# RWKV-7 units of a hybrid decoder block: the products of the two heads are issued in turn

## The chip, the cores and the metric

The kernel runs on one core of a Trainium2 chip. The metric is the device time of one launch in microseconds (us): the median of repeated runs, 2375.93 us before the change (three runs, 2375.08 to 2376.63). All views below come from one profiled execution, which took 2376.5 us. In them PE is the tensor engine (TensorE), PEld its weight loads, DVE the vector engine (VectorE), ACT the scalar engine (ScalarE), POOL is GpSimd, and SP the engine that issues most loads.

## What is computed

One layer of a decoder on a sequence of 512 tokens with 2048 features, in float32. The normalised input is projected by one large matrix; its columns belong to four groups of token mixers: four gated DeltaNet heads (A), four retention heads (B), eight Mamba-2 heads (C) and eight RWKV-7 heads of width 64 (D). The outputs are joined, projected back, and a squared-ReLU MLP follows. The change concerns group D alone:

```python
def _rwkv7_scan(r, decay, k, v, kk, a):
    def step(S, inp):
        r_t, d_t, k_t, v_t, kk_t, a_t = inp
        sa = jnp.einsum('bhvk,bhk->bhv', S, -kk_t)
        S = S * d_t[:, :, None, :] + sa[..., None] * (kk_t * a_t)[:, :, None, :] + v_t[..., None] * k_t[:, :, None, :]
        return S, jnp.einsum('bhvk,bhk->bhv', S, r_t)
    xs = tuple(jnp.moveaxis(t, 1, 0) for t in (r, decay, k, v, kk, a))
    _, y = lax.scan(step, jnp.zeros((Bsz, H, N, N), jnp.float32), xs)
    return jnp.moveaxis(y, 0, 1)
```

## The kernel before

**Stages.** The projection and the token mixers run together until about 890 us; then come the output projection, the two halves of the MLP (each by a scheme with seven block products in place of eight), and the last normalisation. The change is in the first stage.

**Units.** The mixers are cut into twelve units, run in the order D0, A0, D1, A1, C0, D2, A2, C1, D3, A3, B0, B1. A D unit (function `rwkv`) has two RWKV heads: head 0 lies on partitions 0 to 63 of its tiles, head 1 on 64 to 127 (`half`; `rb` is the pair the other way round). The 512 tokens are eight chunks of 64.

**What sets the order.** Each projection block (`proj`) is 48 products of 128x512 (L457), each operand split in two parts, hi and lo (L281 on ScalarE, L282 on VectorE). Every unit is a generator. After every four L457 products (`QUANTUM`) one tick passes; a `yield n` in a unit that has got all its projections means that its next piece comes n ticks later. So TensorE's order is written by hand: pieces of up to two older units stand between the projection products of the next. GpSimd's order is written by hand too. The orders of VectorE, ScalarE and of the load queue are made by a list scheduler from the dependencies, so a change of the program's order can move instructions there.

**Accumulators.** `BK()` gives one of six rotating accumulators (`bk`, `zb`, `xb`, `sb`, `yb`), one bank of 128x512 each; the two accumulators of the projection are apart.

**A D unit behind its projections, with the lines of the profile:** the keys of both heads are transposed, eight per head, into one accumulator per head (L652) and copied by ScalarE to `KT` (L654). Then the products of keys and queries, four chunks to an accumulator (L665), are masked by VectorE into `Ph` (L666), scaled and masked again (L674, L675), and reduced (L679). A recursion of fifteen steps on VectorE (L567 to L569) and a few small products (L692, L713, L720, with L700, L704 and L705 on VectorE between them) invert a triangular matrix. Last comes the loop over chunks: `zb` is the sum of a product with the state `Sx` (L732) and one with `Ph` (L733), copied to `Z` (L734); `xb` (L738) gives the update (L739, L740), `sb` (L749) the new state `Sn` (L752, L754), and `yb` is the sum of L757 and L759, copied to `Y` (L760). In the first chunk there is no state, so L732 and L759 are missing.

**How products stand on the array.** The profile gives rows*columns of the array that a product uses. L652 and L665 use 64 rows (those of the head's partitions) and all 128 columns; L732, L733, L738, L759 and L692 use 64*64; L749 and L757 128*64. A transpose is one record in the profile, a product of float32 operands two.

Of the kernel before, what the change touches and what calls it, by code (L numbers as in the profile page):

```python
# [191 lines left out]
def tile_trunk(ctx: ExitStack, tc: tile.TileContext, ins, out):  # L192
    nc = tc.nc
    V, A, PE, G = nc.vector, nc.scalar, nc.tensor, nc.gpsimd
# [13 lines left out]
    M = lambda n="m": ps.tile([128, 1024], F32, tag="m", name=n, bufs=NM)  # L208
    BK = lambda n="bk": pm.tile([128, 512], F32, tag="bk", name=n)
# [14 lines left out]
    def C(n, a=0, w=None):  # L224

        if n in _L:
            if n not in wide:
                wide[n] = S(n)
                nc.scalar.dma_start(wide[n], ins["wide"][_L.index(n)])
            return wide[n][:, a:a + (w or 512)]  # L230
        return con[:, _C[n][0] + a:_C[n][0] + a + (w or _C[n][1])]
    Pm = lambda n, a=0, w=1: par[:, _P[n][0] + a:_P[n][0] + a + w]

    def bc(ap, shape):
        return ap.broadcast_to(shape)
# [93 lines left out]
    def weights(more=0):  # L329
        ahead(more)  # L330
        w = halves.pop(st["n"])
        st["n"] += 1
        return w
# [239 lines left out]
    def rwkv(j):  # L573
        v3 = lambda q: q.rearrange("p (c t) -> p c t", c=8)
        half = (slice(0, 64), slice(64, 128))
# [4 lines left out]
        bk = BK()  # L580
# [14 lines left out]
        bk = BK()  # L595
# [13 lines left out]
        bk = BK()  # L609
# [11 lines left out]
        AR = M("AR").rearrange("p (c x t) -> p c x t", c=8, x=2)  # L621
        KB = M("KB").rearrange("p (c x t) -> p c x t", c=8, x=2)
# [11 lines left out]
        bk = BK()  # L634
# [7 lines left out]
        bk = BK()  # L642
# [3 lines left out]
        yield 4  # L646

        KT = []
        for h in range(2):
            bk = BK()  # L650
            for c in range(8):
                PE.transpose(bk[:, 64 * c:64 * c + 64], KB[half[h], c], C("i2")[half[h]])  # L652
            kt = v3(S("KT"))
            A.copy(kt, v3(bk))  # L654
            KT.append(kt)
            yield 1

        Ph = []
        for h in range(2):
            p = M("Ph").rearrange("p (c x t) -> p c x t", c=8, x=2)  # L660
            for q in range(2):
                bk = BK()
                b4 = bk.rearrange("p (c x t) -> p c x t", c=4, x=2)
                for c in range(4):
                    PE.matmul(b4[:, c], KB[half[h], 4 * q + c], AR[half[h], 4 * q + c], start=True, stop=True)  # L665
                V.tensor_tensor(p[:, 4 * q:4 * q + 4].rearrange("p c x t -> p c (x t)"),  # L666
                                bk.rearrange("p (c y) -> p c y", c=4),
                                bc(C("rmask").unsqueeze(1), (128, 4, 128)), op=ALU.mult)
                yield 1
            Ph.append(p)  # L670
        rb = (half[1], half[0])
        cm = S("cm")
        for h in range(2):
# [14 lines left out]
        def quad(fn_l, fn_r):  # L688
            bk = v3(BK())
            for c in range(8):  # L690
                for h in range(2):
                    PE.matmul(bk[rb[h], c], fn_l(h, c), fn_r(h, c), start=True, stop=True)  # L692
            return bk
# [4 lines left out]
        bk = quad(lambda h, c: Ph[h][rb[h], c, 0], lambda h, c: X[rb[h], c])  # L698
# [11 lines left out]
        bk, U = v3(BK()), v3(S("U"))  # L710
# [6 lines left out]
        bk = v3(BK())  # L717
# [9 lines left out]
        for c in range(8):  # L727
            Z = E128("Z")[:, 0:64]
            zb = BK("zb")
            for h in range(2):  # L730
                if Sx is not None:
                    PE.matmul(zb[rb[h], 0:64], AR[half[h], c, 0], Sx[half[h]], start=True, stop=False)  # L732
                PE.matmul(zb[rb[h], 0:64], Ph[h][half[h], c, 0], VX[h][half[h], c], start=Sx is None, stop=True)  # L733
            V.tensor_copy(Z, zb[:, 0:64])  # L734
            yield 1
            xb = BK("xb")
            for h in range(2):
                PE.matmul(xb[rb[h], 0:64], XT[rb[h], c], Z[rb[h]], start=True, stop=True)  # L738
            A.activation(VX[0][64:128, c], xb[64:128, 0:64], AF.Copy, scale=nn2[64:128, c:c + 1])  # L739
            V.tensor_scalar(VX[1][0:64, c], xb[0:64, 0:64], nn2[0:64, c:c + 1], None, op0=ALU.mult)  # L740
            if c < 7 and Sx is not None:
                sg = E128("sg")[:, 0:64]
                V.tensor_scalar(sg, Sx, gc[:, c:c + 1], None, op0=ALU.mult)
            yield 2
            Sn = None
            if c < 7:
                sb = BK("sb")
                for h in range(2):
                    PE.matmul(sb[half[h], 0:64], KT[h][:, c], VX[h][:, c], start=True, stop=True)  # L749
                Sn = E128("Sn")[:, 0:64]  # L750
                if Sx is None:
                    V.tensor_scalar(Sn, sb[:, 0:64], gc[:, c:c + 1], None, op0=ALU.mult)  # L752
                else:
                    V.scalar_tensor_tensor(Sn, sb[:, 0:64], gc[:, c:c + 1], sg, op0=ALU.mult, op1=ALU.add)  # L754
            yb = BK("yb")
            for h in range(2):
                PE.matmul(yb[half[h], 0:64], Ph[h][:, c, 1], VX[h][:, c], start=True, stop=Sx is None)  # L757
                if Sx is not None:
                    PE.matmul(yb[half[h], 0:64], AR[half[h], c, 1], Sx[half[h]], start=False, stop=True)  # L759
            A.copy(Y[:, c], yb[:, 0:64])  # L760
            Sx = Sn
            yield 1
# [18 lines left out]
        bk = BK()  # L781
# [402 lines left out]


    units = {"D": rwkv, "A": gdn, "C": ssd, "B": ret}
    active = []

# [284 lines left out]
    for j in range(2 * EARLY):  # L1473
        p, m = j // 2, 1 + j % 2
        h, l = weights(2)
# [205 lines left out]
    for c in range(7):  # L1681
        for s in range(2):
            for m in DORD[c]:
# [3 lines left out]
                for t in range(2):  # L1687
                    if m in (2, 3, 4):
                        x = ht[t + 2 * (m == 4)][s + 2 * (m == 3)]
                    else:  # L1690
                        x = kept[m, s, t]
# [28 lines left out]
    c = 7  # L1720
# [49 lines left out]
```

## Time and profile before

| | |
|---|---|
| median of three runs | 2375.93 us |
| profiled execution | 2376.5 us |
| its span, first to last instruction | 2374.7 us |
| TensorE busy, of the span | 98% |
| VectorE busy, of the span | 75% |
| ScalarE busy, of the span | 43% |
| granted TensorE clock, mean | 0.993 |
| L665, 128 records: busy | 18.5 us |
| L652, 64 records: busy | 5.7 us |
| L757 and L759, 128 and 112 records: busy | 18.5 and 18.2 us |
| L732 and L733, 112 and 128 records: busy | 9.5 and 9.4 us |

A timeline row has the start in the span, the time to the end of the last of the row's instructions, engine, line, operation, output<-inputs, rows*columns of the array, elements, type and count, and in brackets the engine's idle time before it with what ended that. Records of TensorE overlap, so the step from one row's start to the next is what it occupies. A row of the groups has the busy time of all its instructions, the mean of one in ns, and the idle time before them. A busy time is what at least one of the group's instructions covers.

### The profile page before, as it was taken

The page shows a single profiled execution, that of the slowest core. Times are in us where ns is not written, and L with a number is a line of the kernel's source. Part 1 is how long each engine was busy: PE and PEld are TensorE (multiplying, and loading weights), DVE is VectorE, ACT ScalarE, POOL GpSimd, SP SyncE. Part 2 cuts the span into 40 slices and gives each one's busy share as a digit, 9 for nine tenths or more (in the row PEclk, how much of TensorE's full clock was granted, in tenths as well). Part 3 has the DMA queues.
Part 4 walks back from the last instruction along what each step waited for, and adds up shares of the span by engine and source line. Part 5 has one row for each costly group of instructions (what it writes and reads, how often), then busy time and mean ns, then how long its engine had stood idle before and what let it go on. Part 6 is the DMA issues. An engine that isn't in the chain of part 4 may idle for free.

```text
span 2374.7 us, 36713 instructions
## 1 busy us (share of the span) xinstructions
PE 2317.4 (98%) x14690; PEld 1988.6 (84%) x14690; DVE 1773.4 (75%) x2783; ACT 1016.3 (43%) x1480; POOL 195.4 (8%) x270
## 2 busy tenths in 40 slices
PE   6999999999999999998999999999999999999996
PEld 6777778777777788878999999999988888888885
DVE  5685855775584444468888888888888888898898
ACT  5322233333322232354455555555565544445443
POOL 1110201211210210011111100000010000000000
PEclk9999999999999999999999999999999999999998
DMA  5553626563653675564877754444476655656451
GB/s 199 147 142 82 161 70 153 150 159 98 168 144 98 173 195 195 176 218 158 260 216 213 222 160 160 160 160 160 160 276 218 205 169 169 212 174 212 151 199 71
DMA packets 159916, 404.76 MB, mean 170 GB/s; under 512 B 12929, under 2 KB 79489, under 8 KB 158721
## 3 DMA queue, kind: packets, MB, share of 16 engines
q1 hardware_dynamic: 83952, 285.42, 36.9%
q0 software_dynamic: 38912, 77.08, 14.3%
q10 hardware_dynamic: 36880, 39.92, 4.9%
q8 instruction: 115, 1.88, 0.3%
q14 instruction: 57, 0.46, 0.1%
HBM read 355.70 MB, written 113.77 MB: 198 GB/s over the span
## 4 chain that ended last, share of the span: by engine, by line
PE 80%; DVE 9%; issue 6%; DMA 2%; POOL 1%; ACT 1%; SPq 0%; POOLq 0%; DVEq 0%; ACTq 0%
PE acc L457 17%; PE p L1441 8%; PE p L1443 8%; PE p L1442 8%; PE dn L1675 8%; PE dn L1676 8%; PE dn L1674 8%; PE wo L1239 2%; PE wo L1247 2%; PE wo L1240 2%; DVE lo L282 1%; PE acc L481 1%; DVE xi L567 1%; DVE xm L568 1%; DVE lo L1575 1%
## 5 line engine op out<-in xcount | busy, mean ns | idle before, releaser
L1574 ACT CAST hi<-raw 128x1024 fp32r<-128x1024 f32 x224 | 235.0, 1054 | 290.6 <-PE dn L1676 238.2
L1674 PE MATMUL dn<-hi,x 128*128 128x512 f32 x896 | 349.8, 390 | 5.7 <-ACT hi L1574 5.7
L1675 PE MATMUL dn<-lo,x 128*128 128x512 f32 x896 | 350.0, 391 | 2.4 <-DVE lo L1575 2.2
L1676 PE MATMUL dn<-hi,x 128*128 128x512 f32 x896 | 349.3, 390 | 0.0
L281 ACT CAST hi<-raw 128x1024 fp32r<-128x1024 f32 x162 | 169.7, 1049 | 409.5 <-PE acc L457 307.6
L457 PE MATMUL acc<-ah,hi 128*128 128x512 f32 x832 | 336.3, 404 | 0.0
L457 PE MATMUL acc<-al,hi 128*128 128x512 f32 x832 | 335.5, 403 | 0.0
L457 PE MATMUL acc<-ah,lo 128*128 128x512 f32 x832 | 333.7, 401 | 0.0
L1575 DVE TENSOR_TENSOR lo<-raw,hi 128x1024 fp32r<-128x1024 f32 x224 | 272.9, 1223 | 62.6 <-ACT hi L1574 62.2
L1434 ACT CAST hi<-raw 128x1024 fp32r<-128x1024 f32 x216 | 226.6, 1051 | 209.7 <-PE p L1442 149.1
L1435 DVE TENSOR_TENSOR lo<-raw,hi 128x1024 fp32r<-128x1024 f32 x216 | 263.0, 1222 | 70.9 <-ACT hi L1434 70.4
L282 DVE TENSOR_TENSOR lo<-raw,hi 128x1024 fp32r<-128x1024 f32 x160 | 195.3, 1223 | 142.8 <-ACT hi L281 127.5
L1674 PEld LDWEIGHTS dn<-hi,x 128*128 128x128 f32 x896 | 168.7, 188 | 41.5 <-ACT hi L1574 6.5
L1675 PEld LDWEIGHTS dn<-lo,x 128*128 128x128 f32 x896 | 168.7, 188 | 38.8 <-DVE lo L1575 4.0
L1676 PEld LDWEIGHTS dn<-hi,x 128*128 128x128 f32 x896 | 168.7, 188 | 35.0
L457 PEld LDWEIGHTS acc<-ah,hi 128*128 128x128 f32 x832 | 156.4, 188 | 38.5 <-issue 7.4
L457 PEld LDWEIGHTS acc<-ah,lo 128*128 128x128 f32 x832 | 156.4, 188 | 34.7 <-issue 2.9
L457 PEld LDWEIGHTS acc<-al,hi 128*128 128x128 f32 x832 | 156.5, 188 | 32.0 <-issue 1.9
L1432 DVE TENSOR_TENSOR raw<-raw,raw 128x1024 f32<-128x1024 f32 x124 | 151.5, 1222 | 2.8 <-DMA raw<-in_wup_dram 1.1
L1570 DVE TENSOR_TENSOR raw<-raw 128x1024 f32<-128x1024 f32 x64 | 77.7, 1221 | 0.6
L311 POOL TENSOR_TENSOR pace<-pace,mhalf 128x1 f32<-128x1 f32 x64 | 40.2, 628 | 445.2 <-ACT pace L310 445.2
L1443 PE MATMUL p<-s2h,lo 128*128 128x256 f32 x256 | 72.6, 283 | 0.8 <-DVE lo L1435 0.8
(500 smaller groups left out, 5061.8 us busy)
## 6 DMA issues: line engine op xcount, KB each, us to landing
raw<-in_wup_dram SPq DMA_DIRECT2D x136, 512.0 KB, 5.4
t<-in_wdn_dram POOLq DMA_DIRECT2D x128, 512.0 KB, 7.9
raw<-in_win_dram SPq DMA_DIRECT2D x106, 512.0 KB, 3.9
raw<-in_wdn_dram SPq DMA_DIRECT2D x96, 512.0 KB, 4.5
h<-ct ACTq DMA_DIRECT2D x32, 1024.0 KB, 9.6
raw<-t SPq DMA_DIRECT2D x64, 512.0 KB, 4.4
raw<-h SPq DMA_DIRECT2D x56, 512.0 KB, 4.3
raw<-in_wout_dram SPq DMA_DIRECT2D x48, 512.0 KB, 3.7
```

The source lines that it names most:

```text
L282: by.tensor_tensor(l[:, :w], r[:, :w], h[:, :w].bitcast(F32), op=ALU.subtract)
L457: PE.matmul(acc[:w], a, b, start=n == 0, stop=n == 47)
L1434: A.copy(h, r)
L1435: V.tensor_tensor(l, r, h.bitcast(F32), op=ALU.subtract)
L1441: PE.matmul(acc, wh, rh[:, k], start=k == 0, stop=False)
L1442: PE.matmul(acc, wh, rl[:, k], start=False, stop=False)
L1443: PE.matmul(acc, wl, rh[:, k], start=False, stop=k == 7)
L1574: A.copy(h, r[1])
L1575: V.tensor_tensor(l, r[1], h.bitcast(F32), op=ALU.subtract)
L1674: PE.matmul(accs[t], xh, h[:, ws], start=kk == 0, stop=False)
L1675: PE.matmul(accs[t], xh, l[:, ws], start=False, stop=False)
L1676: PE.matmul(accs[t], xl, h[:, ws], start=False, stop=kk == 3)
```

## The change

In `rwkv` the two heads take turns wherever both have the same kind of product. The sixteen transposes to `KT` alternate head by head into two accumulators; the key products alternate in the same way, so that there are two groups of eight products (quarter q of both heads) instead of four groups of four; the ticks between them are put together (`yield 2` twice instead of `yield 1` four times, and one `yield 2` instead of two `yield 1` behind the transposes). In the chunk loop the loop over heads is cut in two, for `zb` and for `yb`: first the first product of both heads, then the second of both. No product is added or left out, and no operand changes.

```diff
         KT = []
+        bks = [BK(), BK()]
+        for c in range(8):
+            for h in range(2):
+                PE.transpose(bks[h][:, 64 * c:64 * c + 64], KB[half[h], c], C("i2")[half[h]])
         for h in range(2):
-            bk = BK()
-            for c in range(8):
-                PE.transpose(bk[:, 64 * c:64 * c + 64], KB[half[h], c], C("i2")[half[h]])
             kt = v3(S("KT"))
-            A.copy(kt, v3(bk))
+            A.copy(kt, v3(bks[h]))
             KT.append(kt)
-            yield 1
-
-        Ph = []
-        for h in range(2):
-            p = M("Ph").rearrange("p (c x t) -> p c x t", c=8, x=2)
-            for q in range(2):
-                bk = BK()
-                b4 = bk.rearrange("p (c x t) -> p c x t", c=4, x=2)
-                for c in range(4):
-                    PE.matmul(b4[:, c], KB[half[h], 4 * q + c], AR[half[h], 4 * q + c], start=True, stop=True)
-                V.tensor_tensor(p[:, 4 * q:4 * q + 4].rearrange("p c x t -> p c (x t)"),
-                                bk.rearrange("p (c y) -> p c y", c=4),
+        yield 2
+
+        Ph = [M("Ph").rearrange("p (c x t) -> p c x t", c=8, x=2) for _ in range(2)]
+        for q in range(2):
+            bks = [BK(), BK()]
+            for c in range(4):
+                for h in range(2):
+                    PE.matmul(bks[h].rearrange("p (c x t) -> p c x t", c=4, x=2)[:, c],
+                              KB[half[h], 4 * q + c], AR[half[h], 4 * q + c], start=True, stop=True)
+            for h in range(2):
+                V.tensor_tensor(Ph[h][:, 4 * q:4 * q + 4].rearrange("p c x t -> p c (x t)"),
+                                bks[h].rearrange("p (c y) -> p c y", c=4),
                                 bc(C("rmask").unsqueeze(1), (128, 4, 128)), op=ALU.mult)
-                yield 1
-            Ph.append(p)
+            yield 2
...
                     PE.matmul(zb[rb[h], 0:64], AR[half[h], c, 0], Sx[half[h]], start=True, stop=False)
+            for h in range(2):
                 PE.matmul(zb[rb[h], 0:64], Ph[h][half[h], c, 0], VX[h][half[h], c], start=Sx is None, stop=True)
...
                 PE.matmul(yb[half[h], 0:64], Ph[h][:, c, 1], VX[h][:, c], start=True, stop=Sx is None)
+            for h in range(2):
                 if Sx is not None:
                     PE.matmul(yb[half[h], 0:64], AR[half[h], c, 1], Sx[half[h]], start=False, stop=True)
```

Lines move a little: L665 becomes L664, L666 L667, and from L733 on a line number is one higher, from L759 on two.

TensorE's order in unit D0, before, from the transposes to the first two groups of key products (between them the projection products of A0; `con` holds the identity, x8 and x4 count program products):

```order
L652 MATMUL bk<-con,KB 128x64 x8
L457 MATMUL acc<-ah_129,hi 128x512
L457 MATMUL acc<-al_133,hi 128x512
L457 MATMUL acc<-ah_129,lo 128x512
L457 MATMUL acc<-ah_129,hi 128x512
L652 MATMUL bk<-con,KB 128x64 x8
L457 MATMUL acc<-al_133,hi 128x512
L457 MATMUL acc<-ah_129,lo 128x512
L457 MATMUL acc<-ah_129,hi 128x512
L457 MATMUL acc<-al_133,hi 128x512
L665 MATMUL bk<-AR,KB 128x128 x4
```

The same place now:

```order
L652 MATMUL bk<-con,KB 128x64 x16
L457 MATMUL acc<-ah_129,hi 128x512
L457 MATMUL acc<-al_133,hi 128x512
L457 MATMUL acc<-ah_129,lo 128x512
L457 MATMUL acc<-ah_129,hi 128x512
L457 MATMUL acc<-al_133,hi 128x512
L457 MATMUL acc<-ah_129,lo 128x512
L457 MATMUL acc<-ah_129,hi 128x512
L457 MATMUL acc<-al_133,hi 128x512
L664 MATMUL bk<-AR,KB 128x128 x8
```

The eight transposes of head 1 moved ahead of four projection products, to those of head 0, and the first group of key products has both heads. The second group of eight stands where the third group of four stood.

TensorE's order in the chunk loop of unit D0, one chunk from `sb` to the next chunk's `zb`, before (VX_905 and VX_906 are the operands of head 0 and head 1):

```order
L749 MATMUL sb<-VX_905,KT 64x64
L749 MATMUL sb<-VX_906,KT 64x64
L757 MATMUL yb<-VX_905,Ph 64x64
L759 MATMUL yb<-Sn,AR 64x64
L757 MATMUL yb<-VX_906,Ph 64x64
L759 MATMUL yb<-Sn,AR 64x64
L457 MATMUL acc<-ah_128,hi 128x512
L457 MATMUL acc<-al_132,hi 128x512
L457 MATMUL acc<-ah_128,lo 128x512
L457 MATMUL acc<-ah_128,hi 128x512
L732 MATMUL zb<-Sn,AR 64x64
L733 MATMUL zb<-VX_905,Ph 64x64
```

And now:

```order
L750 MATMUL sb<-VX_905,KT 64x64
L750 MATMUL sb<-VX_906,KT 64x64
L758 MATMUL yb<-VX_905,Ph 64x64
L758 MATMUL yb<-VX_906,Ph 64x64
L761 MATMUL yb<-Sn,AR 64x64 x2
L457 MATMUL acc<-ah_128,hi 128x512
L457 MATMUL acc<-al_132,hi 128x512
L457 MATMUL acc<-ah_128,lo 128x512
L457 MATMUL acc<-ah_128,hi 128x512
L732 MATMUL zb<-Sn,AR 64x64 x2
L734 MATMUL zb<-VX_905,Ph 64x64
L734 MATMUL zb<-VX_906,Ph 64x64
```

In `yb` the product of head 1 with `Ph` changed places with the state product of head 0; in `zb` the same two kinds changed places.

VectorE's order behind the key products of D0, before (cv, KQ, gs and e belong to unit A0, lo is a split of a weight tile):

```order
L666 TENSOR_TENSOR Ph<-bk,con 128x512
L282 TENSOR_TENSOR lo<-raw,hi 128x1024
L666 TENSOR_TENSOR Ph<-bk,con 128x512
L801 SCALAR_TENSOR_TENSOR cv<-acc,par,cv 128x511
L674 TENSOR_TENSOR Ph<-Ph,n_879 64x8x64
L801 SCALAR_TENSOR_TENSOR cv<-acc,par,cv 128x510
L801 SCALAR_TENSOR_TENSOR cv<-acc,par,cv 128x509
L808 SCALAR_TENSOR_TENSOR KQ<-th,cv 128x4x128
L835 TENSOR_TENSOR gs<-e,con 128x512
L666 TENSOR_TENSOR Ph<-bk,con 128x512
L836 TENSOR_TENSOR e<-e,con 128x512
L666 TENSOR_TENSOR Ph<-bk,con 128x512
```

And now:

```order
L667 TENSOR_TENSOR Ph<-bk,con 128x512 x2
L282 TENSOR_TENSOR lo<-raw,hi 128x1024
L803 SCALAR_TENSOR_TENSOR cv<-acc,par,cv 128x511
L803 SCALAR_TENSOR_TENSOR cv<-acc,par,cv 128x510
L667 TENSOR_TENSOR Ph<-bk,con 128x512
L803 SCALAR_TENSOR_TENSOR cv<-acc,par,cv 128x509
L667 TENSOR_TENSOR Ph<-bk,con 128x512
L674 TENSOR_TENSOR Ph<-Ph,n_879 64x8x64
L810 SCALAR_TENSOR_TENSOR KQ<-th,cv 128x4x128
L837 TENSOR_TENSOR gs<-e,con 128x512
L675 TENSOR_TENSOR cm<-Ph,con 64x512
L838 TENSOR_TENSOR e<-e,con 128x512
```

One multiplication for `Ph` moved ahead of the split, and the other two ahead of KQ and gs. The orders of GpSimd and of the load queue are the same as before, but for line numbers.

## Prediction, made before the changed kernel was timed

> **What bounds the kernel now.** I read the page first (busy time, slices, chain), then the windows, then TensorE's timeline around the touched products, then VectorE's timeline behind them.
>
> ```profile
> span 2374.7 us, 36713 instructions
> PE 2317.4 (98%) x14690; PEld 1988.6 (84%) x14690; DVE 1773.4 (75%) x2783; ACT 1016.3 (43%) x1480; POOL 195.4 (8%) x270
> PE 80%; DVE 9%; issue 6%; DMA 2%; POOL 1%; ACT 1%; SPq 0%; POOLq 0%; DVEq 0%; ACTq 0%
> sum 700.00, PE 691.20 PEld 535.04 DVE 459.25 ACT 213.75 POOL 105.89; mean PE 9.87 PEld 7.64 DVE 6.56 ACT 3.05 POOL 1.51
> ```
>
> The last row is the sum of seventy windows from 100 to 800 us, the stage in which the RWKV units run between the projection products. TensorE (PE) idles 8.8 us of the 700 there, and the chain of work that ended last is 80% PE. So a microsecond taken from PE's queue comes off the end, unless another engine cannot follow.
>
> **The output products (L757, L759): 14.0 us.** A product of float32 operands is two records (passes) in the trace, a transpose one.
>
> ```profile
> 170.06 0.29 PE L757 MATMUL yb<-VX,Ph 128*64 128x64 f32 x4
> 170.28 0.50 PE L457 MATMUL acc<-ah,lo 128*128 128x512 f32 x1
> 172.93 0.33 PE L738 MATMUL xb<-Z,XT 64*64 64x64 f32 x4
> 173.19 0.50 PE L457 MATMUL acc<-al,hi 128*128 128x512 f32 x1
> 175.40 0.28 PE L757 MATMUL yb<-VX,Ph 128*64 128x64 f32 x2
> 175.61 0.33 PE L759 MATMUL yb<-Sn,AR 64*64 64x64 f32 x2
> 175.87 0.33 PE L757 MATMUL yb<-VX,Ph 128*64 128x64 f32 x2
> 176.12 0.33 PE L759 MATMUL yb<-Sn,AR 64*64 64x64 f32 x2
> 176.38 0.50 PE L457 MATMUL acc<-ah,hi 128*128 128x512 f32 x1
> ```
>
> From 175.40 the two kinds take turns. One uses 128 rows by 64 columns of the array, the other 64 by 64, and every turn costs 0.21 to 0.26 us: together 176.38 - 175.40 = 0.98. After the change both L757 come first, as in chunk 0 at 170.06, where four passes end in 170.28 - 170.06 = 0.22. Then come both L759, for which the nearest row is the two heads' 64*64 products L738: 173.19 - 172.93 = 0.26. So 0.48 in place of 0.98, 0.50 saved. A chunk with an earlier state does this: 7 chunks by 4 units = 28 times, **14.0 us**. The only reader of yb, a copy on ScalarE, feeds nothing until the end of the unit.
>
> **The state products (L732, L733): 0.**
>
> ```profile
> 171.42 0.34 PE L732 MATMUL zb<-Sn,AR 64*64 64x64 f32 x4
> 171.58 0.29 PE L733 MATMUL zb<-VX,Ph 64*64 64x64 f32 x4
> 171.80 0.50 PE L457 MATMUL acc<-ah,hi 128*128 128x512 f32 x1
> ```
>
> The program has head 0's L732 and L733, then head 1's. In time all four L732 passes start ahead of any L733: the two heads' 64x64 parts already run beside each other, and reordering them can win nothing. [...]
>
> **The Ph products and the KT transposes (L665, L652): 10.3 and 3.3 us.**
>
> ```profile
> 100.75 0.39 PE L457 MATMUL acc<-ah,lo 128*128 128x512 f32 x1
> 101.07 0.71 PE L652 MATMUL bk<-con,KB 64*128 64x64 f32 x8
> 101.07 0.40 PE L652 MATMUL bk<-con,KB 64*128 64x64 f32 x3
> 101.71 0.50 PE L457 MATMUL acc<-ah,hi 128*128 128x512 f32 x1
> 102.05 0.39 PE L457 MATMUL acc<-al,hi 128*128 128x512 f32 x1
> 104.27 0.40 PE L457 MATMUL acc<-al,hi 128*128 128x512 f32 x1
> 104.60 1.16 PE L665 MATMUL bk<-AR,KB 64*128 64x128 f32 x8
> 104.60 0.71 PE L665 MATMUL bk<-AR,KB 64*128 64x128 f32 x4
> 105.68 0.51 PE L457 MATMUL acc<-ah,lo 128*128 128x512 f32 x1
> 106.03 0.40 PE L457 MATMUL acc<-ah,hi 128*128 128x512 f32 x1
> ```
>
> (The rows with x3 and x4 are the same groups in a window that ends earlier.) Undisturbed projection products (L457) step by about 0.23. Around a Ph group two of them stand 106.03 - 104.27 = 1.76 apart, so a group costs 1.76 - 0.46 = 1.30; its passes step by (1.16 - 0.71)/4 = 0.112, eight make 0.90, and 0.40 is entering and leaving. A KT group costs 102.05 - 100.75 - 0.46 = 0.84, its passes 0.062 each. The change makes one group of sixteen passes out of two of eight: 16 Ph groups become 8, 8 KT groups become 4.
>
> What sixteen alternating passes cost is not in this trace: the two heads use the upper and lower 64 rows, but all 128 columns both. **Lower bound of the gain:** they follow each other; then only entering and leaving is saved, 8 x 0.40 = 3.2 and 4 x (0.84 - 8 x 0.062) = 4 x 0.34 = 1.4. **Upper bound:** they run beside each other; then sixteen take as long as eight (plus some ns), 8 x 1.29 = 10.3 and 4 x 0.83 = 3.3. The nearest row is the alternating pair of heads on 64 rows by 64 columns:
>
> ```profile
> 155.03 1.15 PE L692 MATMUL bk<-XT,U 64*64 64x64 f32 x32 [0.29 <-DVE U L700]
> 156.01 1.10 PE L692 MATMUL bk<-U,XT 64*64 64x64 f32 x32
> ```
>
> 32 passes in 156.01 - 155.03 = 0.98 us, 0.031 each, where L652, also with 64 moving columns and one head, needs 0.062. Two L757 heads, on different columns but the same rows, show it too (four passes in 0.22 with the exit). I take the upper bound, since each dimension by itself seems no obstacle. [...]
>
> Gross: 14.0 + 10.3 + 3.3 = **27.6 us** of PE time.
>
> **What VectorE gives back: 3.9 us.** Behind Ph comes the one stretch of a unit where VectorE (DVE) sets the pace.
>
> ```profile
> 110.00:160.00 50.00, 49.02 (x343) 39.83 (x345) 45.56 (x152) 13.53 (x21) 7.92 (x12) 1.00 0.53 137
> 170.00:220.00 50.00, 50.00 (x413) 35.37 (x413) 25.97 (x70) 15.18 (x35) 2.11 (x3) 1.00 0.26 74
> 107.77 1.23 DVE L282 TENSOR_TENSOR lo<-raw,hi 128x1024 fp32r<-128x1024 f32 x1 [1.29 <-ACT hi L281]
> ...
> 113.29 0.69 DVE L808 SCALAR_TENSOR_TENSOR KQ<-th,cv 128x512 f32<-128x512 f32 x1 [0.76 <-ACT th L807]
> 113.90 0.68 DVE L835 TENSOR_TENSOR gs<-e,con 128x512 f32<-128x512 f32 x1
> ...
> 118.07 1.23 DVE L282 TENSOR_TENSOR lo<-raw,hi 128x1024 fp32r<-128x1024 f32 x1 [0.25 <-ACT hi L281]
> 159.84 0.69 PE L713 MATMUL bk<-X,Ph 32*32 32x32 f32 x32 [0.69 <-DVE X L705]
> L713 PE MATMUL bk<-X,Ph 32*32 32x32 f32 x128 | 2.8, 191 | 3.6 <-DVE XT L569 2.2 <-DVE X L705 1.4
> 788.42 0.49 PE L976 MATMUL yb<-Yc,QT 128*128 128x128 f32 x2 [2.74 <-DVE Yc L964]
> ```
>
> In the windows' rows (stretch, its length, then busy time of PE, its weight loads, DVE and so on) DVE is busy 45.56 of the 50 us from 110 to 160, and at the end of it PE waits for DVE (0.29 at 155.03, 0.69 at 159.84; over the four units 3.6 before L713). PE arrives there 0.83 + 2 x 1.29 = 3.41 us earlier. DVE gains: its packed run starts with the split at 107.77, 0.83 earlier, since the projection product that frees its buffer stands behind the first Ph group; one Ph multiplication of 0.61 (113.90 - 113.29, the step of such an operation) now runs ahead of it, in the gap; the waits of 0.76 and 0.25 go, because other Ph work stands there. That is 2.45, so 0.96 of PE's gain turns into a longer wait in each unit: 4 x 0.96 = 3.9. Bounds: 0 (DVE follows entirely) and 13.6 (none of KT and Ph comes through). The gains at L757 lie in the chunk loop from 170 to 220, where DVE is busy 25.97 of 50, and come through.
>
> Two accumulators are now asked for at once; six rotate, and the second is one whose reader finished several groups before, so I cost that at nothing; uncovered it would be a Ph multiplication, 0.6, in twelve places, 7 us, inside the bound above. The DMA and POOL queues keep their order.
>
> **Sum:** 27.6 - 3.9 = 23.7. The profiled execution took 2376.5 us (span 2374.7, 1.8 around it), 0.6 above the median of 2375.93 of the runs. From the median: **2352.2 us**.
>
> **Rivals.**
> - *Row halves do not overlap* (16%). For: no row shows them. Against: 64*64 and 128*64 pairs both do. Gains 14.0 + 3.2 + 1.4 = 18.6; DVE starts 0.9 - 0.34 = 0.56 later behind the longer first Ph group and gains 1.62 in the stretch, 1.06 against PE's 1.15 per unit, 0.4 lost in all: 18.2, **2357.7**.
> - *DVE swallows KT and Ph whole* (10%): its stretch does not start earlier. For: 9 of 10 busy. Against: its run begins with waits for PE's work. Only 14.0 stays: **2361.9**.
> [...]
> - *Changing the row half empties the array, like changing the shape* (4%), which ends slower. Its price is in the rows
>
> ```profile
> 812.97 0.48 PE L1161 MATMUL ob<-R,qd 64*128 64x128 f32 x2
> 813.38 0.49 PE L1159 MATMUL ob<-vt,PT 128*128 128x128 f32 x2
> 813.80 0.48 PE L1161 MATMUL ob<-R,qd 64*128 64x128 f32 x2
> ```
>
> where each turn takes 0.41 in place of 2 x 0.112 for the same two passes. Eight Ph groups of eight turns would cost 8 x (8 x 0.41 + 0.40) = 29.4 against 16 x 1.30 = 20.8 now, 8.6 lost; 64 KT transposes at half a turn, 0.205 in place of 0.062, lose 9.1 - 1.4 = 7.7. 16.3 lost and 14.0 won: +2.3, **2378.2**. It decides from about 0.39 a turn on. Against it: L692's heads change row half at every product without such a step.
>
> **How the numbers follow.** The forecast has 66%, the rivals 16, 10, 3 and 4, other things 1. The forecast's own range goes from 2346 (no loss at DVE, and the wait of 2.74 us at 788.42 also gone) to about 2356. To leave no more than 2 in 10 outside, the range reaches to the second rival: 2346 to 2362. A measurement of this kernel can tell about 0.2%, 4.8 us, from no change. All cases but the last rival lie more than that below: faster 0.94; the last rival is within 0.2% or, if a turn costs more, above: same 0.04, slower 0.02.
>
> **What would show it.** Right: L757 x4 followed by L761 x4 in 0.48 us; L652 x16 in about 0.7 and L664 x16 in about 1.2 us of busy time; idle before L713 up from 3.6 to 6 or 7 us. Wrong in the Ph step: L664 x16 lasting 2.0 us or more. Wrong in the DVE step: TensorE's idle from 100 to 800 us unchanged, or up by over 10 us. The whole is wrong if the time after the last RWKV unit is not what it was, since nothing there is changed.

## The result, and the profile after

The changed kernel took **2352.36 us** (median of four runs, 2348.97 to 2356.37) beside 2376.28 us (four runs, 2375.08 to 2379.21) for the kernel before: a ratio of **0.9905** with a 95% interval of 0.9893 to 0.9916. The forecast was 2352.2 us in a range of 2346 to 2362. The profiled execution took 2356.37 us and is the slowest of the four, so the trace shows 20.1 us of gain (2376.5 - 2356.37) where the medians show 23.9. Most of what is missing has one place in the trace, below. That the median lies within 0.2 us of the forecast is partly chance, since the four runs lie 7.4 us apart.

The page of the changed kernel, for its span, busy times and the chain of work that ended last by engine:

```profile
span 2354.6 us, 36711 instructions
PE 2290.2 (97%) x14690; PEld 1969.7 (84%) x14690; DVE 1772.2 (75%) x2783; ACT 1016.7 (43%) x1480; POOL 194.8 (8%) x270
PE 78%; DVE 10%; issue 6%; DMA 4%; POOL 1%; ACT 1%; SPq 0%; POOLq 0%; DVEq 0%; ACTq 0%
```

TensorE is busy 2317.4 - 2290.2 = 27.2 us less, with as many instructions. In the chain PE has 2% less, DVE 1% more and DMA 2% more: part of the saved time turned into waits.

The same stretch as before in one window of 700 us (busy time of PE, its weight loads, DVE, ACT and POOL, then granted clock, DMA share and GB/s):

```profile
100.00:800.00 700.00, 685.54 (x4912) 532.83 (x4910) 465.79 (x1205) 216.93 (x406) 107.14 (x141) 1.00 0.53 137
```

PE idles 14.5 us of it; it was 8.8.

The groups of the products that the change reorders (busy time of all, mean ns of one, idle before):

```profile
L758 PE MATMUL yb<-VX,Ph 128*64 128x64 f32 x128 | 9.5, 225 | 0.0
L664 PE MATMUL bk<-AR,KB 64*128 64x128 f32 x128 | 9.3, 285 | 0.0
L761 PE MATMUL yb<-Sn,AR 64*64 64x64 f32 x112 | 9.3, 242 | 0.0
L652 PE MATMUL bk<-con,KB 64*128 64x64 f32 x64 | 2.8, 229 | 0.0
```

All four have half of their earlier busy time (18.5, 18.5, 18.2 and 5.7), and one instruction takes as long as it did (285 and 229 ns in both for L664 and L652). So no single product is faster in the trace: two of them now lie beside each other, and in the output products turns between two shapes are gone as well. TensorE's timeline shows it:

```profile
101.37 0.71 PE L652 MATMUL bk<-con,KB 64*128 64x64 f32 x16
...
104.05 1.16 PE L664 MATMUL bk<-AR,KB 64*128 64x128 f32 x16
...
718.61 0.34 PE L750 MATMUL sb<-VX,KT 128*64 128x64 f32 x4
718.77 0.29 PE L758 MATMUL yb<-VX,Ph 128*64 128x64 f32 x4
718.99 0.33 PE L761 MATMUL yb<-Sn,AR 64*64 64x64 f32 x4
719.25 1.16 PE L902 MATMUL bk<-X,LT 128*128 128x128 f32 x8
```

Sixteen transposes last 0.71 us, as eight did, and sixteen passes for Ph 1.16 us, as eight did. The output products take 719.25 - 718.77 = 0.48 us in place of 0.98.

What PE waited for from 100 to 800 us (in total, times, longest); first the changed kernel, then the row of before that differs most:

```profile
PE bk L692 <- DVE U L700: 4.8, 4, 1.4
PE yb L978 <- DVE Yc L966: 4.7, 2, 4.4
PE bk L713 <- DVE XT L569: 2.2, 2, 1.1
PE bk L713 <- DVE X L705: 1.4, 2, 0.7
PE xb L739 <- DVE Z L735: 0.5, 1, 0.5
PE bk L851 <- DVE xi L567: 0.5, 1, 0.5
```

```profile
PE bk L692 <- DVE U L700: 1.6, 4, 0.8
```

The wait before L713 is what it was, 2.2 + 1.4. The one before L692 grew by 3.2, and L739 waits 0.5 that it did not wait before. At the A units' yb (L978, before L976) a wait of 2.74 us became one of 4.39, and a second one of 0.3 is new, in the stretch of unit D1. The 4.39 and the slow products behind it are the 3 us that the profiled execution lacks. All engines of the changed kernel there, then the same place before the change:

```profile
756.56 0.33 ACTq L229 DMA_DIRECT2D dmask<-in_wide_dram  x1
...
761.78 0.39 PE L457 MATMUL acc<-ah,hi 128*128 128x512 f32 x1
...
765.55 0.69 DVE L1138 TENSOR_TENSOR PT<-bk,dmask 128x512 f32<-128x512 f32 x1 [6.22 <-DMA dmask<-in_wide_dram]
766.16 0.34 DVE L966 TENSOR_SCALAR Yc<-xb,E 128x128 f32<-128x128 f32 x1
766.56 0.80 PE L978 MATMUL yb<-Yc,QT 128*128 128x128 f32 x2 [4.39 <-DVE Yc L966]
767.01 0.77 PE L457 MATMUL acc<-al,hi 128*128 128x512 f32 x1
767.58 0.63 PE L457 MATMUL acc<-ah,lo 128*128 128x512 f32 x1
768.00 0.63 PE L457 MATMUL acc<-ah,hi 128*128 128x512 f32 x1
...
769.62 0.39 PE L457 MATMUL acc<-al,hi 128*128 128x512 f32 x1
```

```profile
780.07 0.33 ACTq L229 DMA_DIRECT2D dmask<-in_wide_dram  x1
...
785.29 0.39 PE L457 MATMUL acc<-ah,hi 128*128 128x512 f32 x1
787.41 0.69 DVE L1136 TENSOR_TENSOR PT<-bk,dmask 128x512 f32<-128x512 f32 x1 [4.57 <-DMA dmask<-in_wide_dram]
...
790.13 0.40 PE L457 MATMUL acc<-al,hi 128*128 128x512 f32 x1
```

A retention unit (B0) asks for its mask when it first needs it, on ScalarE's queue, and VectorE's multiplication with it stands in VectorE's queue ahead of Yc, for which TensorE waits. At the last projection product ahead of the wait the change is 785.29 - 761.78 = **23.5 us** ahead; behind it 788.42 - 766.56 = 21.9, and behind the next products, which step by 0.43 us in place of 0.23, 790.13 - 769.62 = 20.5. From there to the end of the span it changes by 0.4 only (2374.7 - 2354.6 = 20.1). The first projection product, ahead of all RWKV units, starts 0.3 us later here than before (53.46 and 53.16); counted from there, the change is 23.8 us ahead. This start differs from trace to trace, also between traces of one kernel: from 1.8 us later to 2.1 us earlier than before the change, in places that no edit touches.

The windows of the changed kernel at that place, granted clock third from the end:

```profile
766.00:768.00 2.00, 1.44 (x4) 1.26 (x5) 0.80 (x3) 0.21 (x1) 0.00 (x0) 0.52 0.00 0
768.00:770.00 2.00, 2.00 (x7) 1.47 (x5) 0.85 (x2) 0.41 (x1) 0.59 (x1) 0.63 0.00 0
```

So a wait of 4.39 us was followed by some 2.7 us of products (766.56 to 769.28) at about half the clock.

### The profile page after: what moved, and what is told of

Read it like the earlier page. It is cut to its first block, busy times and chain, and to the rows that moved or that the text cites. A ratio compares the mean times of both kernels' runs of the same rounds, so it can differ in the third digit from the quotient of the medians.

```text
span 2354.6 us, 36711 instructions
## 1 busy us (share of the span) xinstructions
PE 2290.2 (97%) x14690; PEld 1969.7 (84%) x14690; DVE 1772.2 (75%) x2783; ACT 1016.7 (43%) x1480; POOL 194.8 (8%) x270
## 3 DMA queue, kind: packets, MB, share of 16 engines
q0 software_dynamic: 38912, 77.08, 14.5%
## 4 chain that ended last, share of the span: by engine, by line
PE 78%; DVE 10%; issue 6%; DMA 4%; POOL 1%; ACT 1%; SPq 0%; POOLq 0%; DVEq 0%; ACTq 0%
PE acc L457 16%; PE p L1443 8%; PE p L1445 8%; PE p L1444 8%; PE dn L1677 8%; PE dn L1678 8%; PE dn L1676 8%; PE wo L1241 2%; PE wo L1242 2%; PE wo L1249 2%; DVE lo L282 1%; PE acc L481 1%; DMA h<-ct 1%; DVE lo L1577 1%; DVE xi L567 1%
## 6 DMA issues: line engine op xcount, KB each, us to landing
h<-ct ACTq DMA_DIRECT2D x32, 1024.0 KB, 10.1
```

## The experiments

The theory at this point: the gain is that of passes lying beside each other, a term for each kind of product, less a wait for VectorE behind the Ph products; the mask's wait is apart from it. The rivals: the zb products have a part in it; the merging of groups is what helps, not the alternation; the waits are a matter of the ticks between pieces; the longer mask wait belongs to the change.

**Output products alone.** The kernel before, with only the loop of yb cut in two:

```diff
             for h in range(2):
                 PE.matmul(yb[half[h], 0:64], Ph[h][:, c, 1], VX[h][:, c], start=True, stop=Sx is None)
+            for h in range(2):
                 if Sx is not None:
```

> The kernel before, with the output products alone cut into two loops over the heads (L757 of both heads, then L759 of both). Theory (the turns between 128*64 and 64*64 cost, and TensorE's time comes off the end): 28 groups by 0.50 us, 14.0 us less than before, about 2362; each group from its first product to what follows it 0.48 us instead of 0.98. Rival (the gain lies in the key products, since VectorE's stretch behind them starts earlier): within 3 us of before.

Measured: 2360.44 us (2359.78 to 2361.48), ratio 0.9942 (0.9927 to 0.9957) to 2373.93 us for the kernel before: 13.5 us. The two groups of yb are busy for 9.5 and 9.3 us, as in the whole change. The start of every projection product, compared with the kernel before, moves ahead by 0.50 us at each of the 28 groups and nowhere else, and falls back by 0.5 where the xb product of the last D unit now waits for Z. 14.0 - 0.5 = 13.5, which the trace shows up to the mask wait (13.6, of it 0.1 from the start): the term has its size.

**Transposes and Ph products alone.** The changed kernel with the loop over chunks as it was:

```diff
-            for h in range(2):
                 PE.matmul(zb[rb[h], 0:64], Ph[h][half[h], c, 0], VX[h][half[h], c], start=Sx is None, stop=True)
...
-            for h in range(2):
                 if Sx is not None:
```

> The changed kernel with the two loops of the chunk loop as before: only the transposes and the key products alternate. Theory: 13.6 us of TensorE time saved, 3.9 given back in a longer wait for VectorE before L692 or L713, 9.7 us less than before, about 2366.5. Rival (VectorE swallows the whole): within 2 us of before. Rival (VectorE follows entirely): 13.6 less, about 2362.5.

Measured: 2365.68 us (2361.85 to 2370.4, eight runs), ratio 0.9967 (0.9956 to 0.9978): 8.3 us. In its trace the start of the last product ahead of the mask wait is 9.75 us earlier than before the change, or 10.1 counted from the first projection product. Then comes a mask wait of 3.37 us with a stretch of slow products behind it, which leaves 7.6. L664 and L652 are busy for 9.3 and 2.8 us, as in the whole change, and the wait before L692 is 4.8 here too, so the 3.2 us given back there belong to this part of the change alone.

**State products alone.** The kernel before with only the loop of zb cut in two.

```diff
                     PE.matmul(zb[rb[h], 0:64], AR[half[h], c, 0], Sx[half[h]], start=True, stop=False)
+            for h in range(2):
                 PE.matmul(zb[rb[h], 0:64], Ph[h][half[h], c, 0], VX[h][half[h], c], start=Sx is None, stop=True)
```

> The kernel before, with the state products alone cut into two loops (L732 of both heads, then L733 of both). Theory (the two heads' parts already run beside each other): no change, within 1.5 us of before, and the step from the first L732 to what follows the group stays at 0.38 us. Rival (matmuls start in program order, so the heads followed one another before): up to 0.12 us by 28, 3.4 us less.

Measured: 2374.6 us (2372.01 to 2379.05, ten runs), ratio 1.0002 (0.9993 to 1.0012). The zb groups are busy for 9.3 and 9.2 us, where they had 9.5 and 9.4, and their step in the trace stays 0.38 us (172.03 to 172.41). This edit is worth nothing that the runs can show. The 0.12 us of the rival is the step of 0.38 less the 0.26 of the four passes of L738 (172.93 to 173.19 before).

**Merged groups without alternation.** The changed kernel with the heads one behind the other in each merged group:

```diff
-        for c in range(8):
-            for h in range(2):
+        for h in range(2):
+            for c in range(8):
                 PE.transpose(bks[h][:, 64 * c:64 * c + 64], KB[half[h], c], C("i2")[half[h]])
...
-            for c in range(4):
-                for h in range(2):
+            for h in range(2):
+                for c in range(4):
```

> The changed kernel with the same merged groups of sixteen, but in each all passes of head 0 ahead of all of head 1: nothing is alternated in the transposes and key products. Theory (overlap comes from alternating, and TensorE looks only a few passes ahead): a key group of sixteen passes lasts about 1.5 us (1.1 alternated, 2.0 with no overlap), a transpose group about 0.9 (0.7 and 1.1); 8 by 0.4 and 4 by 0.2, so some 4 us slower than the changed kernel before what VectorE gives back. Rival (TensorE looks far enough ahead by itself, as in the state products): group times as in the changed kernel, the same time. Rival (only entering and leaving was saved): 2.0 us a group, 8 us slower.

Measured: 2355.68 us (2350.82 to 2359.7), ratio 0.9927 (0.991 to 0.9945). Groups and timeline of this kernel:

```profile
L664 PE MATMUL bk<-AR,KB 64*128 64x128 f32 x128 | 13.7, 285 | 0.0
L652 PE MATMUL bk<-con,KB 64*128 64x64 f32 x64 | 4.1, 229 | 0.0
```

```profile
102.50 1.71 PE L664 MATMUL bk<-AR,KB 64*128 64x128 f32 x16
104.14 0.50 PE L457 MATMUL acc<-ah,lo 128*128 128x512 f32 x1
```

The group takes 1.64 us, between the 1.09 of alternating heads and the 2.0 that passes in file would need by the estimate above. Pass by pass, head 1's first one starts right behind head 0's fifth (6 ns later), ahead of head 0's sixth to eighth in the program: here passes of the other row half start from about four places further on, and with eight of one head in front only part of the two heads overlaps. So alternation is needed for the full gain. It costs TensorE (13.7 - 9.3) + (4.1 - 2.8) = 5.7 us to leave it out, of the 13.8 that the transposes and key products save together (below): the larger part comes from merging already, with the overlap that passes in this order find. Of the 5.7, 1.6 come back as shorter waits before L692 (3.2 in place of 4.8) and 0.5 in unit D1, where the changed kernel loses as much around L978; at the last product ahead of the mask wait, counted from the first projection product, this kernel has lost 3.4 us to the changed one. The medians differ by more (18.3 us of gain beside 23.9), but the four runs of this kernel lie 8.9 us apart.

**More ticks behind the multiplications of VectorE.** If TensorE merely comes too early to L692 and L713, one more group of projection products in front of them fills the wait. The changed kernel with

```diff
         V.tensor_tensor(U, bk, bc(C("rl1").unsqueeze(1), (128, 8, 64)), op=ALU.mult)
-        yield 2
+        yield 3
...
         V.tensor_tensor(X, X, b1, op=ALU.subtract)
-        yield 2
+        yield 3
```

> The changed kernel with one tick (four projection products, 0.93 us) more ahead of the second and of the third small product of the inversion (yield 3 for yield 2 twice, behind U and behind XT and X). Theory (the time given back is VectorE being late there, and other products can fill it): TensorE's idle before L692 and L713 falls from 4.8 + 3.6 us to under 3 us, 4 to 7 us less than the changed kernel. Rival (VectorE sets the pace of the whole stretch): the waits move to the next products, the same time within 2 us.

Measured: 2349.27 us (2348.26 to 2350.69), ratio 0.9889 (0.9872 to 0.9905) to 2374.91: 25.6 us. PE's waits in this kernel from 100 to 800 us:

```profile
PE bk L713 <- DVE xm L568: 2.1, 2, 1.0
PE bk L713 <- DVE XT L569: 1.7, 2, 1.2
PE sb L750 <- DVE VX L741: 1.7, 3, 1.0
PE yb L978 <- DVE Yc L966: 1.6, 2, 1.3
PE bk L692 <- DVE U L700: 1.2, 3, 0.4
PE zb L732 <- DVE Sn L753: 1.1, 2, 0.5
```

The waits before L692 and L713 fall from 8.4 to 5.0, but sb, zb and an A unit's yb now wait instead. At the last product ahead of the mask the kernel is not ahead of the changed one (1.5 us behind, of which 1.1 lie ahead of the first projection product). So VectorE sets the pace of that stretch, and the ticks only choose where TensorE stands still. What is shorter in this trace than in the first one of the changed kernel is the mask wait, 0.33 us with no slow products behind it: the mask landed in 4.9 us.

**The mask asked for earlier.** The changed kernel with one line more at the start of the retention unit, ahead of its first multiplication:

```diff
         qr = q4(rot((yield from proj())))
+        C("dmask")
         qd = q4(S("qd"))
```

> The changed kernel with the decay mask of unit B0 (dmask) loaded at the start of the unit instead of at its first use; the load costs ScalarE's queue one issue either way. Theory (the wait of 4.39 us before L978 is the mask's transfer, and the slow projection products behind it follow from the long wait): that wait goes, the L457 behind it step by 0.23 again instead of 0.43 us, 3 to 5.5 us less than the changed kernel, and the runs lie closer together. Rival (the wait is VectorE's backlog): it stays, the same time.

Measured: 2348.08 us (2347.94 to 2350.48), ratio 0.9888 (0.9873 to 0.9902): 26.8 us less than the kernel before in the same set, where the changed kernel had 23.9 in its own. No wait for the mask is left (0.3 us of Yc itself), there are no slow products, and beside the start nothing else moves in the trace. Together with the ticks above:

> The ticks of e5 and the early mask of e6 together on the changed kernel. Theory: their gains add, 8 to 12 us less than the changed kernel, about 2342. Rival (one wait behind two causes): no more than the larger of the two.

Measured: 2349.58 us (2348.43 to 2354.18), ratio 0.9895 (0.9881 to 0.991), 25.3 us less: no better than the mask alone. So what the ticks seemed to gain was the same wait; whether they make the mask land sooner, or it did so by itself in those runs, was not settled.

**One turn of the array's shape more.** To price a turn, the changed kernel issues the yb products with the state between sb and the yb products with Ph, so that 128*64, 64*64 and 128*64 follow each other in 24 chunks in which 128*64 came twice in a row:

```diff
                     PE.matmul(sb[half[h], 0:64], KT[h][:, c], VX[h][:, c], start=True, stop=True)
+                yb = BK("yb")
+                for h in range(2):
+                    if Sx is not None:
+                        PE.matmul(yb[half[h], 0:64], AR[half[h], c, 1], Sx[half[h]], start=True, stop=False)
...
             for h in range(2):
-                if Sx is not None:
-                    PE.matmul(yb[half[h], 0:64], AR[half[h], c, 1], Sx[half[h]], start=False, stop=True)
+                PE.matmul(yb[half[h], 0:64], Ph[h][:, c, 1], VX[h][:, c], start=Sx is None, stop=True)
```

> The changed kernel with the two products of yb in the other order: the state products of both heads (64*64) stand between the sb products and the Ph products (both 128*64), so the array's shape turns once more in each of 24 chunks; the heads stay side by side. Theory (a turn costs by itself, 0.15 us more for the first pass behind it): 24 by 0.15 = 3.6 us slower than the changed kernel. Rival (only heads that follow one another cost): the same time.

Measured: 2357.52 us (2355.99 to 2361.16), ratio 0.9927 (0.9912 to 0.9942): 17.4 us less than before the change, where the changed kernel had 23.9. The same chunk as in the timeline of the changed kernel at 718.61:

```profile
722.91 0.34 PE L754 MATMUL sb<-VX,KT 128*64 128x64 f32 x4
723.18 0.33 PE L758 MATMUL yb<-Sn,AR 64*64 64x64 f32 x4
723.44 0.34 PE L765 MATMUL yb<-VX,Ph 128*64 128x64 f32 x4
723.70 1.16 PE L906 MATMUL bk<-X,LT 128*128 128x128 f32 x8
```

The three groups take 723.70 - 722.91 = 0.79 us in place of 719.25 - 718.61 = 0.64, so one turn costs about 0.15. The projection products fall back by 0.15 at 20 of the 24 places. At the other four, one in each unit, they fall back by 0.40: there 64*64 products of an A unit follow yb directly, and with the state products no longer last a turn lies there too, and the overlap of those two 64*64 groups, which the changed kernel has in its trace (L939 of the A unit starts 0.01 us behind L761, at 733.75), is lost: at 738.73 L943 starts 0.26 behind yb. That makes 20 x 0.15 + 4 x 0.40 = 4.6 us, where 3.6 were expected; the trace has 4.5 at the last product ahead of the mask wait, counted from the first projection product. The old order of yb had three turns where the new one has one, so by my estimate some 0.3 (2 x 0.15) of its 0.50 us are turns and 0.2 the heads lying beside each other.

Between the heads' row halves no such cost shows: sixteen passes of L664 that change the half at every product last 1.16 us, as eight of one head did.

The wait for the mask was 2.42 us in this trace, and slow products followed it too:

```profile
769.71 0.49 PE L982 MATMUL yb<-Yc,QT 128*128 128x128 f32 x2 [2.42 <-DVE Yc L970]
...
771.24 0.63 PE L457 MATMUL acc<-ah,lo 128*128 128x512 f32 x1
771.67 0.63 PE L457 MATMUL acc<-ah,hi 128*128 128x512 f32 x1
```

```profile
772.00:774.00 2.00, 2.00 (x21) 1.25 (x21) 0.84 (x3) 1.15 (x2) 1.74 (x4) 0.50 0.00 0
```

Before the change a longer wait, 2.74 us, had no slow products behind it (the granted clock is 1.00 in the window from 788 to 790 us).

**The changed kernel beside the one with the mask earlier, on one chip.**

> The changed kernel once more, on one chip beside the next one. If the wait for the mask behind the last RWKV unit, with the clock behind it, makes part of its spread, its times lie some 3 to 7 us apart again and its median about 3 us above the next kernel's: 2349 to 2354 us.

> The changed kernel with the mask's load asked for earlier, beside the changed kernel on the same chip. If the wait for the mask costs time in most executions: median 2348 us, 2 to 5 us under the changed kernel, and runs within 3 us of each other. If only the one profiled execution of the changed kernel had a long wait: medians within 2 us of each other and the same spread.

Measured: the changed kernel 2352.57 us (2348.97 to 2353.91), ratio 0.9903 (0.9887 to 0.992); with the mask earlier 2346.58 us (2346.19 to 2349.67), ratio 0.9879 (0.9864 to 0.9894), both to 2376.0. The difference of 6.0 us is larger than the 2 to 5 forecast, and the spread 3.5 where less than 3 was; three of its four runs lie below all of the changed kernel's, one among them. The two profiled executions are only 2.8 us apart (2348.97 and 2346.19), of which 1.2 lie ahead of the first projection product, so no trace shows the whole of the 6.0. In this second trace of the changed kernel:

```profile
755.39 0.34 ACTq L229 DMA_DIRECT2D dmask<-in_wide_dram  x1
761.94 0.69 DVE L1138 TENSOR_TENSOR PT<-bk,dmask 128x512 f32<-128x512 f32 x1 [3.78 <-DMA dmask<-in_wide_dram]
...
762.94 0.49 PE L978 MATMUL yb<-Yc,QT 128*128 128x128 f32 x2 [1.95 <-DVE Yc L966]
763.50 0.39 PE L457 MATMUL acc<-ah,lo 128*128 128x512 f32 x1
763.73 0.40 PE L457 MATMUL acc<-ah,hi 128*128 128x512 f32 x1
```

The same program, and the mask is there in 6.5 us instead of 9.0 after its issue; TensorE waits 1.95 in place of 4.39, and the products behind step by 0.23. This execution took 2348.97 us, the other 2356.37: of the 7.4 us between them 2.4 are the wait, 1.3 the slow products, 1.2 lie in the first 35 us and 2.4 behind the mixers. From issue to landing, and PE's wait, in the nine traces in which the mask is asked for at its first use:

| kernel | landing, us | wait, us | difference |
|---|---|---|---|
| changed, first trace | 9.0 | 4.39 | 4.6 |
| transposes and Ph alone | 8.0 | 3.37 | 4.6 |
| before | 7.3 | 2.74 | 4.6 |
| one turn more | 7.0 | 2.42 | 4.6 |
| state products alone | 6.9 | 2.28 | 4.6 |
| output products alone | 6.8 | 2.2 | 4.6 |
| merged, not alternating | 6.7 | 2.08 | 4.6 |
| changed, second trace | 6.5 | 1.95 | 4.6 |
| more ticks | 4.9 | 0.33 | 4.6 |

The wait is the landing time less 4.6 us in every kernel, with the change and without: it depends on how long this one load of 256 KB took in that execution. The changed kernel's two traces lie on either side of the one before, so that the longer wait belongs to the change falls. Why the landing varies from 4.9 to 9.0 us was not settled.

## Why the prediction was right, point by point

- **yb, 14.0 us**: 28 times 0.50, alone and in the whole. Right. The two causes (turns some 0.3, overlap 0.2) were not told apart in the prediction; its 0.21 to 0.26 us for a turn is the whole step from one group to the next, of which the turn by itself is 0.15.
- **zb, 0**: right (0.38 us a group before and with the edit alone, ratio 1.0002).
- **Ph 10.3 and KT 3.3, the upper bound**: right. Two row halves that both use all 128 columns overlap in full: sixteen passes of L664 last 1.16 us and sixteen of L652 0.71, as eight did. By the steps of the projection products around the groups both together save 3.4 to 3.5 us a unit, 13.8 in all, where 13.6 were forecast. The rival that the halves do not overlap falls, and so does the one that prices a turn of the row half like one of the shape; the latter would have shown groups of 3.7 us (8 x 0.41 + 0.40). What it calls emptying the array is in the records an overlap of 0.07 us at a turn of the shape (812.97 + 0.48 - 813.38 before), where two groups of one shape overlap by 0.18 (718.61 + 0.34 - 718.77 in the changed kernel).
- **Two row halves in one accumulator** (that they wait for each other is the rival with a chance of 3%): L761 takes the two heads' passes into one yb in 0.26 us, as L738 does, so they do not wait here. These two heads also use different columns of the array; the transposes and key products, which share their columns, write to two accumulators, and one accumulator was not tried for them.
- **Sum of PE time, 27.6**: 27.2 by the busy times.
- **VectorE gives back 3.9**: the mechanism holds, the size holds in part by chance, and the place does not. In unit D0 the multiplication U (L700) starts at 152.18 in place of 154.29, 2.4 us earlier counted from the first projection product, where 2.45 were forecast, and TensorE comes to the stretch 3.5 us earlier, where 3.41 were. But the loss of 1.07 us is at L692 and not at L713, where 3 were forecast: L692 stands ahead of L713 and waits for U, and behind that wait TensorE comes to L713 with no more lead over VectorE than before. D2 and D3 lose 1.07 and 1.09 in the same way. D1, whose L692 waited 0.8 before the change too, waits no longer than it did; it loses 0.5 earlier, around L978, which the prediction does not have. A further 0.5 came at L739, from the yb part, in a chunk loop for which the prediction had no wait. In idle time that is 3.2 + 0.3 + 0.5, and 0.1 at L851: 4.0 in all.
- **Sum, 23.7**: 23.5 at the last product ahead of the mask wait, 23.8 counted from the first projection product, and 23.7 in the second trace of the changed kernel.
- **The wait of 2.74 us at the mask**: the prediction counted it only as one that may go. It moves by itself between executions, 1.95 and 4.39 us in the two traces of the changed kernel, and behind some of them TensorE is slow for a while. The medians of several runs (23.9 and 23.4 us of gain in the two sets) agree with the sum; the one profiled execution alone, with 20.1, would have made the sum look 3.6 us too high. With runs 5 to 7 us apart, the medians alone could not confirm the sum to a few tenths; the two traces carry that.
- **Nothing changes behind the last RWKV unit**: right up to the mask wait and again behind it. By the wording of the prediction's last sign, the 3.0 us lost there in the first trace would have spoken against the whole; in the second trace the same kernel gained 0.8 there, and 2.0 more behind the mixers. The sign could not tell the change from what differs between executions of one program.

## What to carry to other kernels

Products that use different row halves of the array should alternate one by one in the program where one half has more than a few passes in a row (here sixteen passes take 1.09 us in turn and 1.64 in two blocks of eight), and products of one shape should stand together (a turn costs 0.15 us here): what is saved is the overlap, and each turn between shapes. Where the passes overlapped already, as in zb, the same edit won nothing (ratio 1.0002). When TensorE arrives earlier at a chain on another engine, look for the loss at the first wait of that chain; the sum can be right where the place is not. A constant that is loaded at its first use made a wait here that varies between executions (0.33 to 4.39 us in nine traces); asking for it some 55 us earlier (issued at 701 in place of 757) lowered the median by 6.0 us on one chip (2.9 in the earlier sets, 26.8 us of gain beside 23.9) and gave the best kernel of this study. The wait and the slow products behind it make 5.7 us in the first trace of the changed kernel and 1.95 in the second.

## What was not expected of the hardware

- Passes for another row half started ahead of earlier passes in the program, from about four places on (in the kernel with merged blocks head 1's first starts 6 ns behind head 0's fifth; 1.64 us for two blocks of eight, against 1.09 alternating).
- A turn between 128*64 and 64*64 cost 0.15 us (at 20 places of 24, in the kernel with one turn more).
- After waits of 4.39, 3.37 and 2.42 us TensorE ran for a while at half its clock (0.52 and 0.50 in windows of 2 us in the first and the third case; products step by 0.43 in place of 0.23 in all three), and after waits of 2.74, 2.28 and less it did not. The slow products begin 4.4 us after the wait began, or earlier, in the first case (L978 at 766.56 takes 0.80 where it takes 0.49 behind the waits of 1.95, 2.08 and 0.33), 4.7 in the second, behind five products at full speed, and 3.3 in the third. So the length of the wait alone does not decide, and what does was not settled.
